# A hybrid transformer layer on one core: a small tile ahead of the feed-forward weights' buffers is made 96 bytes wider

## The chip, the core and the metric

The kernel runs on one core of one Trainium2 chip. A core has a matrix engine (TensorE; its matmuls are PE in the profile, its weight loads PEld), a vector engine (VectorE, DVE), a scalar engine (ScalarE, ACT), a third elementwise engine (GpSimd, POOL) and a queue that issues the transfers (SyncE, SP). They work on a local memory of 128 partitions; matmuls write to a separate accumulation memory (PSUM). The metric is the device time of one execution in microseconds, lower is better.

## The reference, cut to what matters

One layer of a diffusion backbone: 512 latent tokens and 256 context tokens of width 2048. Attention and a recurrence share one input and one output projection; then comes the feed-forward part, and a last norm:

```python
x = x + g1 * (jnp.concatenate([attn, rw], axis=-1) @ w_out)
x = x + g2 * swiglu(modulate(rmsnorm(x, norm2_g), sh2, sc2), ffn_w1, ffn_w3, ffn_w2)
...
def swiglu(h, w1, w3, w2):
    return (jax.nn.silu(h @ w1) * (h @ w3)) @ w2
```

Here h is 512 x 2048, w1 and w3 are 2048 x 5632, w2 is 5632 x 2048, all in 32-bit floats.

## The kernel before

Every large matrix product is made in three passes. Each factor is split into a high part, rounded to the matrix engine's reduced 32-bit format (F32R), and a low part, the rest; the helper `mm3` (lines 110, 113 and 114) issues three matmuls into one PSUM tile: high weights by high input, high weights by low input, low weights by high input. A matmul has a stationary operand of 128 x 128 (the weights, 512 bytes per partition, brought in by a weight load of its own) and a moving operand of 128 x 512 (the input, 2048 bytes per partition). Every matmul has its weight load, the second one of a triple too, though its weights are those of the first.

The weights of the feed-forward part come through `split2` (lines 1257 to 1266): a transfer fills one of four `raw` buffers (L1262), ACT casts it to `whi` (L1264, two buffers), and DVE subtracts, which gives `wlo` (L1265, two buffers). `raw`, `whi` and `wlo` are tiles of the pool `wf`. The input's parts `ahi` and `alo` are tiles of 16 x 512 per partition in the pool `xp`.

The feed-forward part goes in four rounds (`FCH`) over the hidden width. In a round, 11 blocks of w1 and w3 are made one after the other: per block 2 PSUM tiles `ps_u` with 16 steps of three matmuls each, so 96 matmuls a block and 1056 a round. ACT and DVE make the gated product of the two, split into `ghi` and `glo` (pool `gp`). Then come 16 tiles `ps_d` of the product with w2, of 11 steps of three matmuls, so 528 matmuls a round; DVE adds each to `x1`. In the first round DVE also works off rows of the modulation (`arow`, which use `raw` buffers). In the first block of the first round (L1283 on) the input `ahi`, `alo` is still being made. After the fourth round come a norm and 16 output transfers.

Two earlier stages use `mm3` with the same shapes: the input projection (`ps_z`; input `hhi` and the tiles `lo`, weights `whi` and `wlo` of the pool `wp`), and the last part of the output projection (`ps_o`; weights and input are slices of `ahi` and `alo`).

Within a pool, tiles lie one after the other in the order in which they are first made, each rounded up to a multiple of 32 bytes, and pools that are open together are stacked on each other. In the built program of the kernel before, the tiles that matter lie at these bytes of every partition:

| stage | stationary operand: start byte | modulo 128 | modulo 512 | moving operand: start byte | modulo 128 | modulo 512 |
|---|---|---|---|---|---|---|
| `ps_z` | `whi` 131008, 135104; `wlo` 139200, 143296 | 64 | 448 | `hhi` 49088; `lo` from 81856 on | 64 | 448 |
| `ps_o` | slices of `ahi` 49088 and `alo` 81856 | 64 | 448 | the same two tiles | 64 | 448 |
| `ps_u` | `whi` 153696, 159328; `wlo` 164960, 170592 | 96 | 96 | `ahi` 49088; `alo` 81856 | 64 | 448 |
| `ps_d` | `whi` and `wlo` as in `ps_u` | 96 | 96 | `ghi` 176224; `glo` 198752 | 96 | 96 |

One step of the contraction moves the stationary operand on by 512 bytes and the moving one by 2048, so both columns of remainders hold for every step. `gs2` lies at 126912 (64 bytes wide); after it in the same pool come three tiles of 16 bytes and two buffers `th` of 2048 bytes, and then `wf` begins with `raw` at 131168.

Of the kernel before, what the change touches and what calls it, by code (L numbers as in the profile page):

```python
# [10 lines left out]
F32 = mybir.dt.float32  # L11
# [9 lines left out]
P = 128  # L21
D = 2048
KT = D // P
# [40 lines left out]
def hybrid_layer_kernel(ctx: ExitStack, tc: tile.TileContext, xT, ctxT, pcol, ada_w, ada_t, w_in, lora_up, w_out, w13, w2,  # L64
# [14 lines left out]
    def pc(name, i=0, n=1):  # L79
        o = PC[name][0]  # L80
        return par[:, o + i:o + i + n]
# [652 lines left out]
    with ExitStack() as rc:  # L734
# [465 lines left out]
        wk = fc.enter_context(tc.tile_pool(name="wk", bufs=2, reuse_waits="tile"))  # L1200
# [52 lines left out]
    with fc:  # L1253
# [11 lines left out]
                eng.tensor_tensor(lo[:, :n], raw[:, :n], hi[:, :n].bitcast(F32), op=ALU.subtract)  # L1265
            return hi, lo

        gs2 = wk.tile([P, KT], F32, name="gs2", bufs=1)
        nc.vector.scalar_tensor_tensor(gs2, modT[:, 64:80, 0], 1.0, pc("n2g", 0, 16), op0=ALU.add, op1=ALU.mult)
        rs = ms.rstd(ps_f.tile([P, T], F32, tag="o", name="ps_rs"))  # L1270
        for k in range(KT):
# [177 lines left out]
```

## Time and profile before

| | |
|---|---|
| three runs | 3333.99 us median, 3332.64 to 3337.11 |
| the profiled execution | 3328.19 us |
| its span, first to last instruction | 3326.4 us |
| mean granted clock of TensorE over the span | 0.974 of full speed |
| busy share of PE, PEld, DVE, ACT, POOL | 95%, 74%, 52%, 35%, 17% |
| the feed-forward part | from 1830 us to 3304.5 us, then 21.9 us of norm and output |

The busy time of an engine is the time in which at least one of its instructions runs. Matmuls overlap in the engine: a duration runs from the issue of a matmul to its modelled end, so a matmul of 389 ns can be followed by the next one 227 ns after its start. What a run of matmuls costs is therefore read from the distance of their starts, or from a stretch without idle time divided by the number of its matmuls.

### The profile page before, as it was taken

Reading aid. Unit: us, or ns where it says so; the run is one execution under the profiler, and the core shown is the slowest. Engines: PE = TensorE matmul, PEld = TensorE weight load, DVE = VectorE, ACT = ScalarE, POOL = GpSimd, SP = SyncE. Lnnn points to the kernel's source line nnn. Section 1 sums busy time; section 2 is a strip of 40 time slices with the busy share of each in tenths; the row PEclk is TensorE's granted clock in tenths of the full one; section 3 lists DMA queues with packets and bytes.
Section 4 is the critical chain, followed back from the end, with each engine's and each line's share of the span. In section 5 each row is a group of like instructions: output and inputs, shape, how many; then the busy total and the mean of one; then the engine's idle time right before and its main releaser. Section 6 shows DMA issues by size and latency. Waiting matters only on the chain.

```text
span 3326.4 us, 49781 instructions
## 1 busy us (share of the span) xinstructions
PE 3161.6 (95%) x19840; PEld 2468.2 (74%) x19840; DVE 1743.5 (52%) x2906; ACT 1161.0 (35%) x2007; POOL 561.0 (17%) x597
## 2 busy tenths in 40 slices
PE   8989889989998999999997999999999999999997
PEld 4576557767775777777776788888888888888886
DVE  3377764576656777888885653323333232323233
ACT  4213333444344555555553422212221222112221
POOL 0000000253427344434433100000000000000011
PEclk9999999999999999999998999999999999999999
DMA  9675552354536345455465353322232223222232
GB/s 326 242 237 173 182 165 77 108 144 125 138 102 187 105 125 156 141 151 152 127 189 174 128 193 125 103 85 94 92 107 89 95 92 107 94 88 92 93 111 79
DMA packets 270920, 448.41 MB, mean 135 GB/s; under 512 B 109408, under 2 KB 156768, under 8 KB 270688
## 3 DMA queue, kind: packets, MB, share of 16 engines
q1 hardware_dynamic: 270688, 445.22, 42.9%
q8 instruction: 157, 2.57, 0.3%
q14 instruction: 75, 0.61, 0.1%
HBM read 383.52 MB, written 61.60 MB: 134 GB/s over the span
## 4 chain that ended last, share of the span: by engine, by line
PE 60%; DVE 4%; DMA 2%; POOL 1%; issue 1%; SPq 1%; ACT 0%; DVEq 0%; ACTq 0%; POOLq 0%
PE ps_u L114 10%; PE ps_u L113 10%; PE ps_u L110 10%; PE ps_d L113 5%; PE ps_d L110 5%; PE ps_d L114 5%; PE ps_x L852 2%; PE ps_m L982 2%; PE ps_y L863 2%; PE ps_op L110 2%; PE ps_i L901 2%; PE ps_op L114 1%; PE ps_op L113 1%; PE ps_i L907 1%; PE ps_w L971 1%; PE ps_c L1008 1%
## 5 line engine op out<-in xcount | busy, mean ns | idle before, releaser
L1264 ACT ACTIVATE whi<-raw 128x1024 fp32r<-128x1024 f32 (+1 forms) x240 | 275.0, 1146 | 1109.0 <-PE ps_u L113 603.8
L1265 DVE TENSOR_TENSOR wlo<-raw,whi 128x1024 fp32r<-128x1024 f32 (+1 forms) x238 | 317.9, 1336 | 501.2 <-ACT whi L1264 500.5
L114 PE MATMUL ps_u<-ahi,wlo 128*128 128x512 f32 x1408 | 563.0, 400 | 1.2 <-DVE wlo L1265 1.2
L113 PE MATMUL ps_u<-alo,whi 128*128 128x512 f32 x1408 | 556.1, 395 | 0.9 <-DVE alo L1280 0.9
L110 PE MATMUL ps_u<-ahi,whi 128*128 128x512 f32 x1408 | 552.6, 393 | 4.6 <-ACT whi L1264 2.9
L113 PEld LDWEIGHTS ps_u<-alo,whi 128*128 128x128 f32 x1408 | 265.0, 188 | 70.5 <-DVE alo L1280 1.6
L110 PEld LDWEIGHTS ps_u<-ahi,whi 128*128 128x128 f32 x1408 | 265.2, 188 | 69.1 <-ACT whi L1264 4.2
L114 PEld LDWEIGHTS ps_u<-ahi,wlo 128*128 128x128 f32 x1408 | 265.1, 188 | 62.9 <-DVE wlo L1265 2.0
L205 POOL TENSOR_TENSOR sq<-sq 128x512 f32<-128x512 f32 x22 | 40.8, 1855 | 1428.1 <-ACT sq L201 1427.8
L113 PE MATMUL ps_d<-glo,whi 128*128 128x512 f32 x704 | 273.3, 389 | 0.0
L110 PE MATMUL ps_d<-ghi,whi 128*128 128x512 f32 x704 | 273.3, 389 | 0.0
L114 PE MATMUL ps_d<-ghi,wlo 128*128 128x512 f32 x704 | 273.2, 389 | 0.0
L110 PE MATMUL ps_z<-hhi,whi 128*128 128x512 f32 x544 | 230.7, 424 | 7.6 <-DVE r__3128 L309 4.0
L114 PE MATMUL ps_z<-hhi,wlo 128*128 128x512 f32 x544 | 220.1, 405 | 16.8 <-DVE wlo L106 16.8
L113 PE MATMUL ps_z<-lo,whi 128*128 128x512 f32 x544 | 219.5, 403 | 0.0
L171 DVE SCALAR_TENSOR_TENSOR arow<-arow,siluB 128x1024 f32<-128x1024 f32 x128 | 156.4, 1223 | 116.2 <-DMA arow<-ada_t 115.6
L1315 DVE SCALAR_TENSOR_TENSOR x<-ps_d,modT,x 128x512 f32<-128x512 f32 x64 | 48.1, 751 | 299.8 <-PE ps_d L114 299.8
L893 POOL TENSOR_TENSOR bdB<-XY,mk 64x256 f16<-64x256 f32 x192 | 149.3, 777 | 171.7 <-DVE XY L854 156.0
L106 DVE TENSOR_TENSOR wlo<-raw,whi 128x1024 fp32r<-128x1024 f32 x80 | 106.3, 1329 | 92.3 <-ACT whi L105 92.1
L110 PEld LDWEIGHTS ps_d<-ghi,whi 128*128 128x128 f32 x704 | 132.1, 188 | 27.6
L114 PEld LDWEIGHTS ps_d<-ghi,wlo 128*128 128x128 f32 x704 | 132.1, 188 | 27.5
L113 PEld LDWEIGHTS ps_d<-glo,whi 128*128 128x128 f32 x704 | 132.1, 188 | 27.4
(624 smaller groups left out, 5770.4 us busy)
## 6 DMA issues: line engine op xcount, KB each, us to landing
raw<-w SPq DMA_DIRECT2D x176, 512.0 KB, 3.5
arow<-ada_t SPq DMA_DIRECT2D x128, 512.0 KB, 4.2
raw<-w SPq DMA_DIRECT2D x64, 704.0 KB, 4.1
raw<-w_in SPq DMA_DIRECT2D x72, 512.0 KB, 4.1
ada<-ada_w SPq DMA_DIRECT2D x64, 512.0 KB, 6.7
p1d<-pr SPq DMA_DIRECT2D x64, 256.0 KB, 2.8
XB<-bkd SPq DMA_DIRECT2D x96, 128.0 KB, 3.2
pr<-p1d SPq DMA_DIRECT2D x48, 256.0 KB, 3.2
```

Of the source, the lines that this page charges most:

```text
L106: nc.vector.tensor_tensor(lo, raw, hi.bitcast(F32), op=ALU.subtract)
L110: mm = nc.tensor.matmul(ps, lhsT=whi, rhs=hhi, start=first, stop=False)
L113: nc.tensor.matmul(ps, lhsT=whi, rhs=hlo, start=False, stop=False)
L114: nc.tensor.matmul(ps, lhsT=wlo, rhs=hhi, start=False, stop=last)
L171: nc.vector.scalar_tensor_tensor(a, a, 1.0, siluB[:, 1024 * h:1024 * h + 1024], op0=ALU.mult, op1=ALU.mult, accum_out=macc[:, j - 32, h:h ...
L852: nc.tensor.matmul(px[:, u, :], lhsT=AL[:, d, s_ + u, :], rhs=XB[:, d, s_ + u, :], start=True, stop=True)
L863: nc.tensor.matmul(py[m, u, :n], lhsT=XB[:, d, u, 64 * h:64 * h + P][:, m], rhs=GRz[h][:, d, u, :n], start=True, stop=True)
L893: nc.gpsimd.tensor_tensor(diag(B[l], h, d), ab[h][:, d], lm(l, h, d), op=ALU.mult)
L901: nc.tensor.matmul(ps[:, d, u, :], lhsT=lhs[:, d, u, :], rhs=rhs[:, d, u, :], start=True, stop=True)
L982: nc.tensor.matmul(pm[m, u, :n], lhsT=WT[e][h][:, d, u, m], rhs=YB[h][:, d, u, :n], start=True, stop=True)
L1264: nc.scalar.activation(hi[:, :n], raw[:, :n], AF.Copy)
L1265: eng.tensor_tensor(lo[:, :n], raw[:, :n], hi[:, :n].bitcast(F32), op=ALU.subtract)
```

## The change

The tile `gs2` (16 scales of the second norm per partition) is allocated with 24 further elements of 4 bytes, and only its first 16 elements are used, as before. No instruction is added, removed or given another shape or operand.

```diff
-        gs2 = wk.tile([P, KT], F32, name="gs2", bufs=1)
+
+        gs2 = wk.tile([P, KT + 24], F32, name="gs2", bufs=1)[:, :KT]
```

`gs2` is then 160 bytes wide in place of 64, a multiple of 32 in both cases. All that lies behind it moves up by 96 bytes: the three small tiles and `th` in `wk`, all of `wf` (`raw`, `whi`, `wlo`) and all of `gp` (`ghi`, `glo`). Their starts go from 96 to 64 modulo 128 (`whi`, `wlo`, `ghi` and `glo` from 96 to 192 modulo 512). `x1`, `ahi` and `alo` lie ahead of it and stay.

## Rows read from the trace of the kernel before

**Rows 1.** Page, parts 1 and 4: busy time, and the chain that ended last.

```profile
PE 3161.6 (95%) x19840; PEld 2468.2 (74%) x19840; DVE 1743.5 (52%) x2906; ACT 1161.0 (35%) x2007; POOL 561.0 (17%) x597
...
PE 60%; DVE 4%; DMA 2%; POOL 1%; issue 1%; SPq 1%; ACT 0%; DVEq 0%; ACTq 0%; POOLq 0%
PE ps_u L114 10%; PE ps_u L113 10%; PE ps_u L110 10%; PE ps_d L113 5%; PE ps_d L110 5%; PE ps_d L114 5%; PE ps_x L852 2%; PE ps_m L982 2%; PE ps_y L863 2%; PE ps_op L110 2%; PE ps_i L901 2%; PE ps_op L114 1%; PE ps_op L113 1%; PE ps_i L907 1%; PE ps_w L971 1%; PE ps_c L1008 1%
```

**Rows 2.** Busy time by stretch, first round: first block, other ten blocks.

```profile
core 0: us, PE busy (x) PEld busy (x) DVE busy (x) ACT busy (x) POOL busy (x), PEclk, DMA share, GB/s
1830.03:1863.08 33.05, 28.09 (x99) 20.56 (x100) 23.67 (x35) 21.57 (x28) 9.80 (x7) 0.87 0.09 32
1863.08:2086.38 223.30, 223.30 (x958) 179.65 (x957) 101.11 (x129) 52.60 (x60) 0.00 (x0) 1.00 0.51 166
```

**Rows 3.** Busy time by stretch: ps_d and ps_u in turn, end of the span.

```profile
2086.38:2206.10 119.72, 119.72 (x529) 99.10 (x528) 38.17 (x33) 22.34 (x18) 0.00 (x0) 1.00 0.27 91
2206.10:2452.52 246.42, 246.42 (x1058) 198.24 (x1057) 74.54 (x76) 57.65 (x66) 0.00 (x0) 1.00 0.30 97
...
2938.37:3184.78 246.41, 246.41 (x1057) 198.23 (x1056) 74.52 (x76) 57.64 (x66) 0.00 (x0) 1.00 0.30 97
3184.78:3304.50 119.72, 119.72 (x529) 99.10 (x528) 36.94 (x32) 29.12 (x31) 29.28 (x14) 1.00 0.21 70
3304.50:3326.40 21.90, 3.94 (x25) 3.47 (x23) 14.45 (x32) 0.63 (x1) 0.00 (x0) 0.62 0.52 192
```

**Rows 4.** Groups by line and shape, 1863 to 3304 us: matmuls and weight loads.

```profile
line engine op names shapes xcount | busy us, mean ns | idle before us <-releasers
L114 PE MATMUL ps_u<-ahi,wlo 128*128 128x512 f32 x1376 | 549.1, 399 | 0.5 <-DVE wlo L1265 0.5
L113 PE MATMUL ps_u<-alo,whi 128*128 128x512 f32 x1375 | 541.8, 394 | 0.0
L110 PE MATMUL ps_u<-ahi,whi 128*128 128x512 f32 x1375 | 539.0, 392 | 0.0
L110 PE MATMUL ps_d<-ghi,whi 128*128 128x512 f32 x704 | 273.3, 389 | 0.0
L113 PE MATMUL ps_d<-glo,whi 128*128 128x512 f32 x703 | 272.9, 389 | 0.0
L114 PE MATMUL ps_d<-ghi,wlo 128*128 128x512 f32 x703 | 272.8, 389 | 0.0
```

**Rows 5.** Timeline of PE in the input projection: start us, us, line, operands.

```profile
874.52 0.39 PE L110 MATMUL ps_z<-hhi,whi 128*128 128x512 f32 x1
874.75 0.39 PE L113 MATMUL ps_z<-lo,whi 128*128 128x512 f32 x1
...
877.92 0.39 PE L110 MATMUL ps_z<-hhi,whi 128*128 128x512 f32 x1
```

**Rows 6.** The tile ps_o: duration ns min/median/max, first and last start.

```profile
L113 PE MATMUL ps_o<-alo,ahi x27: 389/389/628, 1800.7 to 1819.8; 128*128 128x512 f32 x27
L114 PE MATMUL ps_o<-ahi,alo x27: 387/389/628, 1801.2 to 1820.0; 128*128 128x512 f32 x27
```

**Rows 7.** Groups by line and shape: casts and subtractions of both weight paths.

```profile
L106 DVE TENSOR_TENSOR wlo<-raw,whi 128x1024 fp32r<-128x1024 f32 x80 | 106.3, 1329 | 92.3 <-ACT whi L105 92.1
...
L1265 DVE TENSOR_TENSOR wlo<-raw,whi 128x1024 fp32r<-128x1024 f32 x174 | 213.8, 1229 | 457.5 <-ACT whi L1264 456.8
L1264 ACT ACTIVATE whi<-raw 128x1024 fp32r<-128x1024 f32 x176 | 186.5, 1060 | 743.1 <-PE ps_u L113 570.7 <-issue 134.0 <-PE ps_d L113 37.5
```

**Rows 8.** Waits, 1863 to 3304 us: total us, times, longest.

```profile
ACT whi L1264 <- PE ps_u L113: 594.3, 139, 4.5
...
DVE arow L171 <- DMA arow<-ada_t: 46.4, 26, 3.7
```

**Rows 9.** The tile raw, 1826 to 3304 us: its transfers, issue to landing.

```profile
DMA to landing us min/median/max: 3.3/3.6/6.2
```

## The prediction

> **What bounds the kernel now.** I read the page first. PE is busy for 95% of the span, and the chain that ended last runs through PE for 60%; of that the feed-forward matmuls alone make some 45% (three lines of `ps_u` at 10% each, three of `ps_d` at 5%) [rows 1]. The change touches only what lies behind `gs2`, so I then cut the feed-forward part into its stretches, with the busy time of each engine. What is to be seen there: but for the first block, PE's busy time equals the length of every stretch to 0.01 us, at a granted clock of 1.00 (the upper level, 2.4 GHz), while DVE and ACT are busy for a half and less [rows 2, 3]. From 1863 to 3304.5 us the time is therefore the number of matmuls times the distance between their starts, and nothing else.
>
> That distance is not the same in the two halves of a round. A `ps_u` stretch has 1056 matmuls (11 blocks of 96, from the code; the counts in the rows also take in a matmul or two at the edges) and takes 246.42 us: 233.35 ns a matmul. A `ps_d` stretch has 528 and takes 119.72 us: 226.74 ns [rows 3]; the three full stretches of the one kind and the four of the other agree to 0.01 us. Shapes, types, clock and weight loads are alike. The groups by line say the same in durations: 392, 394 and 399 ns for the three matmuls of a `ps_u` step, 389 ns for each of the three of `ps_d` [rows 4]. The excess over 389 adds up to 18 ns a step, and the distances give 3 x 6.61 = 19.8 ns; I take the distances.
>
> So 6.61 ns a matmul are lost in `ps_u`, and the question is to what. The table of addresses offers one answer: in `ps_u` the weights start at 96 modulo 128 bytes and the input at 64, in `ps_d` both start at 96. Two earlier stages are the control, because they share with `ps_u` the place of the input (bytes 49088 and 81856 on) and the same helper, but have weights at 64. In the input projection 15 matmuls in a row start from 874.52 to 877.92 us [rows 5]: 3.40 us / 15 = 226.7 ns, as in `ps_d`. In the last part of the output projection the low parts' matmuls have a median of 389 ns [rows 6]. `ps_z` also has 16 steps a tile, as `ps_u` has, so the number of steps is not what sets the two apart. Three stages with one offset cost 226.7 ns or 389 ns, whether that offset is 64 or 96; the one stage with two offsets costs more. I read this as reads of one operand that get in the way of the other's when they are not in step, since the next weights are loaded while the input streams; the trace shows the cost, not that reason.
>
> **The change part by part.**
>
> *`ps_u`, all but the first block.* The weights move from 96 to 64 modulo 128, where `ahi` and `alo` are. Matmuls concerned: 957 in the first round (1056 less the 99 that start by 1863.08 us [rows 2]) and 3 x 1056 = 3168 in the others, 4125 in all. They take 223.30 + 246.42 + 246.42 + 246.41 = 962.55 us now [rows 2, 3]. At the distance of `ps_d` and `ps_z` they would take 4125 x 226.74 ns = 935.30 us. Gain: 27.25 us. Nothing waits in these stretches, so PE gets all of it, and everything behind moves up with it. Bounds: no gain, if the offset is not the reason; and no more than this, since the trace has no `mm3` stage whose 512-column matmuls come at less than 226.7 ns in a run.
>
> *`ps_u`, the first block.* PE is busy for 28.09 of 33.05 us at a mean granted clock of 0.87 [rows 2] and waits for the input and the weights in between. 99 x 6.61 ns = 0.65 us is the most that can come back; I take 0, since that block ends with its last weights.
>
> *`ps_d`.* `whi`, `wlo`, `ghi` and `glo` all move by 96 bytes, so they go on sharing one offset, now 64 instead of 96. `ps_z` has 64 for both and the same distance. I take 0; the bounds are 0 as far as 64 and 96 are concerned.
>
> *Casts, subtractions and transfers at the new addresses.* These are hidden behind the matmuls. The nearest row for buffers at 64 is the path of the input projection, where the subtraction takes 1329 ns against 1229 here [rows 7]; there is other work on DVE there, and I take no difference. If the 100 ns were due to the address: the cover is the time for which ACT waits for a buffer to come free, 594.3 us in 139 waits, 4.3 us each [rows 8]. A half block (24 matmuls) gets shorter, from 24 x 233.35 = 5.60 us to 5.44 us, and the cast, the subtraction and one row of the modulation on DVE (1.06 + 1.23 + 1.23 us) still fit in it. Without that cover, all 176 subtractions of 1024 elements would cost 17.6 us. The transfers take 3.6 us from issue to landing, at most 6.2 [rows 9], with four `raw` buffers ahead; DVE's 26 waits for `arow` (46.4 us) [rows 8] are off the path, PE having no idle time there. Nothing more is asked of the transfers but 3% more rate. No instruction is added.
>
> *Waits on older tiles.* A tile waits until those that held its bytes before are released. By the addresses, each moved tile overlaps the same earlier tiles in its old and its new place, so no wait comes or goes.
>
> Sum: 3328.19 - 27.25 = 3300.94 us for an execution like the profiled one. That one is 5.8 us (0.17%) below the median of the three runs, for reasons that lie outside this part; so against the median, 3333.99 - 27.25 = **3306.7 us**, 0.8% faster.
>
> **The rivals.**
>
> *No change: the address has no part in it.* The Trainium skill speaks for this one, on the page "SBUF — State Buffer", section "Who interferes with whom": TensorE has two read ports of its own, one for the moving operand and one for weight loads, and never waits on anyone. By that rule the sum would be 0 and the time 3334.0 us. The rows speak against it, for 233.35 and 226.74 ns stand in one and the same part of the kernel, at one clock, over thousands of matmuls [rows 3, 4]; something tells them apart, and in `ps_z` the number of steps, the place of the input and the shapes are those of `ps_u`. Against my reading: `ps_u` differs from the others also in that its PSUM tiles alternate in pairs, and in where its weights lie at large. 3334.0 us.
>
> *Part of it.* The third matmul of a step has an excess of 10 ns in its duration, the first 3 and the second 5 [rows 4]. If one kind of pairing is cured and another is not, 3 to 15 of the 18 ns remain: a gain of a sixth to five sixths, 4.5 to 22.7 us; in the middle 3320 us.
>
> *Slower: the offsets must agree modulo 512, not 128.* All three good stages agree modulo 512 too (448 and 448, or 96 and 96), a weight tile being 512 bytes wide. After the change the weights are at 192 and the input at 448: 256 apart, farther from agreement than now (160). The trace has no stage with that distance. If it makes all three matmuls of a step as dear as the dearest is now, 10 ns over `ps_d` instead of a mean excess of 6 ((3 + 5 + 10) / 3) [rows 4], each of the 4125 costs 4 ns more: +16.5 us, 3350.5 us. It decides as soon as the distance between starts in `ps_u` is above 233.35 ns. For it speaks only that the rows can't tell 128 from 512; against it, that a rule modulo 64, 128 or 256 would fit the rows as well and give the full gain, and that even modulo 512 a distance of 256 may be harmless or only cost a part.
>
> **How the numbers follow.** The full gain 0.78; part of it 0.07; no change 0.08; slower 0.07. Differences under 0.2% (6.7 us) are about what a measurement of this kernel can't tell from no change. Faster then takes the full gain and nearly all of the partial one, 0.84; same takes no change and the smallest partial ones, 0.09; slower 0.07. The range has to hold the full gain with the spread of the runs (1.4 us below the median, 3.1 above it) and the upper bound of the first block: 3306.7 - 1.4 - 0.65, with some 2 us for another set of runs, gives 3302; above, 3309.8 for the highest run, and on to 3318 for partial gains from 16 us up. That leaves out the other partial cases, no change and slower, 2 in 10.
>
> **What would show it.** In the profile after: `ps_u` stretches of 239.4 us in rounds two to four (1056 x 226.74) and near 217 us for the ten blocks of the first; all three `ps_u` groups at 389 ns; `ps_d` stretches still at 119.7 us; the first block still about 33 us; PE without idle time in between, and ACT's waits for `ps_u` shorter by about 0.16 us each. Wrong it would be if `ps_u` keeps 392, 394 and 399 ns (the address is not the reason), if the three change unequally (it is, but not by this remainder alone), if `ps_d` gets dearer, or if the matmuls get faster and idle time appears before `whi` or `wlo`.

## The result, and the profile after

The changed kernel takes 3306.79 us (median of four runs, 3305.69 to 3311.38) against 3334.01 us before; the ratio is 0.9921, with a 95% interval of 0.9905 to 0.9936. So it is faster by 0.8%, and the time is that of the forecast, 3306.7 us. That the two agree to 0.1 us is luck, since runs of either kernel spread over more than 4 us; what bears the forecast out is the stretches below.

The execution of the changed kernel that was profiled is the slowest of its four (3311.38 us, span 3309.6 us): its feed-forward part begins at 1840.76 us in place of 1830.03. The instructions ahead of that point are the same in both kernels and their tiles have not moved. In the profiles shown below the same point lies between 1830 and 1850 us, also for kernels that differ only behind it. I therefore compare stretches of the feed-forward part, which repeat to some 0.02 us, and not spans.

Busy time by stretch in the profile after, cut as in [rows 2, 3] (first block; the other ten blocks of the first round; then `ps_d` and `ps_u` in turn; the end):

```profile
core 0: us, PE busy (x) PEld busy (x) DVE busy (x) ACT busy (x) POOL busy (x), PEclk, DMA share, GB/s
1840.76:1873.83 33.07, 28.25 (x100) 21.04 (x101) 23.70 (x35) 21.55 (x28) 9.78 (x7) 0.85 0.10 32
1873.83:2090.76 216.93, 216.93 (x958) 179.54 (x957) 100.96 (x129) 52.60 (x60) 0.00 (x0) 1.00 0.51 170
2090.76:2210.44 119.68, 119.68 (x529) 99.10 (x528) 38.14 (x33) 22.34 (x18) 0.00 (x0) 1.00 0.27 92
2210.44:2449.80 239.36, 239.36 (x1057) 198.20 (x1056) 74.51 (x76) 57.53 (x66) 0.00 (x0) 1.00 0.30 100
...
2928.52:3167.88 239.36, 239.36 (x1058) 198.20 (x1056) 74.51 (x76) 57.52 (x66) 0.00 (x0) 1.00 0.30 100
3167.88:3287.56 119.68, 119.68 (x529) 99.10 (x528) 36.92 (x32) 29.08 (x31) 29.21 (x14) 1.00 0.21 70
3287.56:3309.60 22.04, 4.07 (x25) 3.60 (x23) 14.44 (x32) 0.63 (x1) 0.00 (x0) 0.57 0.51 190
```

Here is the whole gain. Each full `ps_u` stretch went from 246.42 to 239.36 us, 226.67 ns a matmul instead of 233.35, and the ten blocks of the first round from 223.30 to 216.93 us. PE still has no idle time in these stretches. The rest stands where it was: `ps_d` 119.68 us (119.72 before), the first block 33.07 us (33.05), the end 22.04 us (21.90). The feed-forward part and the end together went from 1496.4 to 1468.8 us, which is 27.5 us.

The groups by line of the profile after, 1874 to 3288 us, answer to [rows 4]:

```profile
L113 PE MATMUL ps_u<-alo,whi 128*128 128x512 f32 x1375 | 534.9, 389 | 0.0
L114 PE MATMUL ps_u<-ahi,wlo 128*128 128x512 f32 x1375 | 534.9, 389 | 0.0
L110 PE MATMUL ps_u<-ahi,whi 128*128 128x512 f32 x1375 | 534.9, 389 | 0.0
L113 PE MATMUL ps_d<-glo,whi 128*128 128x512 f32 x704 | 273.2, 389 | 0.0
```

The three matmuls of a `ps_u` step, 392, 394 and 399 ns before, have become alike and as short as those of `ps_d`. What hides behind them did not move. The first row is from the waits of the profile after over the same stretch, the second from its groups by line and shape; they answer to [rows 7, 8]:

```profile
ACT whi L1264 <- PE ps_u L113: 571.2, 139, 4.4
```

```profile
L1265 DVE TENSOR_TENSOR wlo<-raw,whi 128x1024 fp32r<-128x1024 f32 x174 | 213.7, 1229 | 437.9 <-ACT whi L1264 437.2
```

ACT waits 0.17 us less for each buffer (571.2 us in 139 waits, 594.3 before), which is what a half block got shorter by. The subtraction takes 1229 ns at the new address too.

### The profile page after: what moved, and what is told of

Read it like the earlier page. It is cut to its first block, busy times and chain, and to the rows that moved or that the text cites. A ratio compares the mean times of both kernels' runs of the same rounds, so it can differ in the third digit from the quotient of the medians.

```text
span 3309.6 us, 49781 instructions
## 1 busy us (share of the span) xinstructions
PE 3140.8 (95%) x19840; PEld 2470.5 (75%) x19840; DVE 1742.7 (53%) x2906; ACT 1160.5 (35%) x2007; POOL 561.2 (17%) x597
## 4 chain that ended last, share of the span: by engine, by line
PE 59%; DVE 4%; DMA 2%; POOL 2%; issue 1%; ACT 1%; SPq 0%; DVEq 0%; ACTq 0%; POOLq 0%
PE ps_u L114 10%; PE ps_u L113 10%; PE ps_u L110 10%; PE ps_d L110 5%; PE ps_d L113 5%; PE ps_d L114 5%; PE ps_m L982 2%; PE ps_x L852 2%; PE ps_y L863 2%; PE ps_op L110 2%; PE ps_i L901 2%; PE ps_op L114 1%; PE ps_op L113 1%; PE ps_w L971 1%; PE ps_i L907 1%; PE ps_c L1008 1%
## 5 line engine op out<-in xcount | busy, mean ns | idle before, releaser
L114 PE MATMUL ps_u<-ahi,wlo 128*128 128x512 f32 x1408 | 549.4, 390 | 1.2 <-DVE wlo L1265 1.2
```

Of the source, the lines that this page charges most:

```text
L114: nc.tensor.matmul(ps, lhsT=wlo, rhs=hhi, start=False, stop=last)
```

## The experiments

The profile after shows that the move took the excess away. It doesn't show which remainder counts, whether the same would happen in another stage, or which pairs of operands must agree. All kernels below move buffers by widening tiles, as the change does. "Distance" is the start of the weights less the start of the input, and a stage is called free when its matmuls start 226.7 ns apart, as those of `ps_d` did before. Apart from the first and the last two, these kernels ran once, so their stretches are compared and not their whole times. In each fence the first row is a full `ps_u` stretch (1056 matmuls), the second a full `ps_d` stretch (528), from the view by stretch: us, PE's busy time with the number of its instructions, granted clock, share of the DMA engines, GB/s.

**The first product's distance put into the second** (the kernel before, with this edit):

```diff
-        ghi = gp.tile([P, FPC, T], F32R, name="ghi")
-        glo = gp.tile([P, FPC, T], F32R, name="glo")
+        ghi = gp.tile([P, FPC * T + 32], F32R, name="ghi")[:, 24:24 + FPC * T].rearrange("p (k t) -> p k t", t=T)
+        glo = gp.tile([P, FPC * T + 32], F32R, name="glo")[:, 24:24 + FPC * T].rearrange("p (k t) -> p k t", t=T)
```

> The kernel before, with the inputs of the second product (ghi, glo) moved up by 96 bytes, so that its weights start 32 bytes past its input modulo 128, as those of the first product do. First theory, the offset between weights and input sets the distance of the matmuls' starts in any stage: a full ps_d stretch goes from 119.72 to 528 x 233.35 ns = 123.2 us, its three kinds to 392, 394 and 399 ns, the kernel from 3334.0 to 3348 us (four stretches of 3.5 us). Second theory, the dearer matmuls belong to the stage ps_u itself (its PSUM tiles, or where its buffers lie at large): ps_d stays at 119.7 us and 389 ns, the kernel at 3334 us.

```profile
2225.17:2471.58 246.41, 246.41 (x1057) 1.00 0.30 97
2471.58:2594.78 123.20, 123.20 (x529) 1.00 0.26 89
```

`ps_d` went to 123.20 us, the predicted 123.2, and the kernel to 1.0034 of the time before (interval 1.0020 to 1.0048); the four stretches of 3.5 us are 14 us or 1.0042, which lies in it. The second theory falls: a stage that the change never touched gets as dear as `ps_u` was, by a move of its inputs alone. It is the relation of the two addresses, not the stage. One thing was not expected: the three kinds of matmul of `ps_d` became 396, 395 and 397 ns, not 392, 394 and 399. Widening `ghi` by 128 bytes also put `glo` 128 further on modulo 256; I took no notice of that, since I thought in remainders of 128. In this kernel and the next three, the distance that is stated for `ps_d` holds modulo 128 only.

**64 and 96**: `gs2` wider by 32 bytes, `ghi` and `glo` shifted by 32 as in the first edit.

> gs2 wider by 32 bytes: in ps_u the weights start 64 bytes past the input modulo 128; ghi and glo moved up by a further 32: in ps_d the weights start 96 past the input (that is 32 ahead of it). If only equality modulo 128 is free: a full ps_u stretch near 246.4 us as before, a ps_d stretch near 123.2 us. If modulo 64 is what counts: ps_u 239.4 us, as after the change, and ps_d 123.2 us. If the stage itself is the reason: 246.4 and 119.7 us.

```profile
2213.39:2455.11 241.72, 241.72 (x1058) 1.00 0.31 99
2455.11:2578.29 123.18, 123.18 (x529) 1.00 0.27 89
```

**96 and 64**: the same with 64 and 64.

> gs2 wider by 64 bytes and ghi and glo moved up by a further 64: the same two distances exchanged, 96 in ps_u and 64 in ps_d. If only equality modulo 128 is free: ps_u near 246.4 us, ps_d near 123.2 us. If modulo 64 is what counts: ps_u 246.4, ps_d 119.7 us. Were a distance of 96 to cost otherwise than one of 32, ps_u here and ps_d of the kernel with 64 and 96 must show the same size for each matmul.

```profile
2228.04:2474.44 246.40, 246.40 (x1058) 1.00 0.31 97
2474.44:2596.09 121.65, 121.65 (x529) 1.00 0.27 90
```

Modulo 64 is refuted by both: at a distance of 64 neither stage is free. It is cheaper there than elsewhere, 241.72 / 1056 = 228.9 ns and 121.65 / 528 = 230.4 ns, against 233.3 at 96 in both stages. So "any distance costs the same" is wrong as well. It is not 64 as such that is cheap: modulo 512 the distance in `ps_u` is 192 here, and one of 64 costs 233.3 ns in a kernel further down.

**128 and 112**: `gs2` wider by 224 bytes, `ghi` and `glo` shifted by 16.

> gs2 wider by 224 bytes: in ps_u weights and input agree modulo 128 but are 128 apart modulo 256; ghi and glo moved up by a further 16: in ps_d the weights start 112 past the input (16 ahead of it). If modulo 128 is what counts: ps_u 239.4 us, as after the change; if modulo 256: ps_u dearer than that, up to 246.4 us or more. For ps_d: if any distance costs the same, 123.2 us; if the cost grows with the distance, between 119.7 and 123.2 us; if units of 32 bytes decide, 119.7 us or 123.2 us and nothing between.

```profile
2219.29:2464.69 245.40, 245.40 (x1058) 1.00 0.30 97
2464.69:2586.71 122.02, 122.02 (x530) 1.00 0.27 90
```

This is the run that changes the reading. Weights and input of `ps_u` agree modulo 128, as in the changed kernel, and the stretch still takes 245.40 us (232.4 ns a matmul). Agreement modulo 128 is not enough. `ps_d` came to 122.02 us, between the free value and the dear one; since `ghi` lies 16 bytes past the weights and `glo` 144, the run can't say which of the three forecasts for it holds.

**Agreement modulo 512, and 128 once more.** From here on the inputs' and weights' tiles are widened by 512 bytes when they are shifted, so that the distance holds for all of a stage's operands.

```diff
-        gs2 = wk.tile([P, KT], F32, name="gs2", bufs=1)
+        gs2 = wk.tile([P, KT + 88], F32, name="gs2", bufs=1)[:, :KT]
...
+        ghi = gp.tile([P, FPC * T + 128], F32R, name="ghi")[:, 32:32 + FPC * T].rearrange("p (k t) -> p k t", t=T)
+        glo = gp.tile([P, FPC * T + 128], F32R, name="glo")[:, 32:32 + FPC * T].rearrange("p (k t) -> p k t", t=T)
```

> gs2 wider by 352 bytes: in ps_u weights and input agree modulo 512 (the change has them 256 apart); ghi and glo moved up by 128: in ps_d they agree modulo 128 and are 128 apart modulo 256. If agreement modulo 256 is what counts: ps_u 239.4 us, ps_d dearer than 119.7 us, near 528 x 232.4 ns = 122.7 us. If modulo 128: 239.4 and 119.7 us. If modulo 512 were better still than 256: ps_u under 239.3 us.

```profile
2208.30:2447.67 239.37, 239.37 (x1057) 1.00 0.31 100
2447.67:2570.86 123.19, 123.19 (x529) 1.00 0.27 90
```

Agreement modulo 512 gives what 256 gives (239.37 and 239.36 us). A distance of 128, now the same for `ghi` and `glo` and in the other stage, costs the full 123.19 us. Modulo 128 is refuted twice.

**32 and 64; 96 and 16**: `gs2` wider by 384 and 448 bytes, `ghi` and `glo` shifted by 448 and 496.

> gs2 wider by 384 bytes and ghi, glo moved up by 448: in ps_u the weights start 32 bytes past the input modulo 512, in ps_d 64 past. If agreement modulo 256 alone is free, both are dearer than 226.7 ns a matmul: ps_u between 241 and 247 us, ps_d between 120.8 and 123.5 us. If the sign of the distance matters (weights ahead or behind), one of these small distances past the input could be as good as 0 or better: ps_u at or under 239.4, ps_d at or under 119.7 us.

```profile
2215.15:2461.54 246.39, 246.39 (x1058) 1.00 0.30 97
2461.54:2584.74 123.20, 123.20 (x529) 1.00 0.27 89
```

> gs2 wider by 448 bytes and ghi, glo moved up by 496: in ps_u the weights start 96 bytes past the input modulo 512, in ps_d 16 past. If agreement modulo 256 alone is free: ps_u between 241 and 247 us, ps_d between 120.8 and 123.5 us. If units of 32 bytes decide, 16 is free or as dear as 32 and nothing between. If the cost shrinks with the distance, ps_d lies between 119.7 and what 64 costs.

```profile
2218.60:2466.00 247.40, 247.40 (x1057) 1.00 0.30 97
2466.00:2590.93 124.93, 124.93 (x529) 1.00 0.26 87
```

No small distance past the input is as good as none, and the cost does not shrink with the distance: 16 bytes are the dearest case of all, 124.93 / 528 = 236.6 ns, so units of 32 bytes don't decide either. Both stretches of this last kernel are above the ranges that were expected (247 and 123.5 us). Together, for the distances that hold for all operands, in ns a matmul (stretch over number of matmuls):

| distance modulo 512 | 0 | 16 | 32 | 64 | 96 | 128 or 384 | 160 | 192 | 224 | 256 |
|---|---|---|---|---|---|---|---|---|---|---|
| `ps_u` | 226.7 | | 233.3 | | 234.3 | 232.4 | 233.3 | 228.9 | 233.3 | 226.7 |
| `ps_d` | 226.7 | 236.6 | | 233.3 | | 233.3 | | | | |

(160 is the kernel before, 256 the change; `ps_u` and `ps_d` at 384 are the two runs with 128.) Only 0 and 256 are free among those tried.

**The low weights alone off by 32** (the changed kernel, with `wlo` starting 32 bytes into a tile widened by 512, and `ghi`, `glo` shifted by 32):

```diff
-            lo = wf.tile([P, WT], F32R, tag="wlo", name="wlo")
+            lo = wf.tile([P, WT + 128], F32R, tag="wlo", name="wlo")[:, 8:8 + WT]
```

> The changed kernel with the low parts of the weights alone moved up by 32 bytes, and ghi, glo too. In ps_u the high weights agree with both inputs and the low ones are 32 past them; in ps_d the low weights agree and the high ones are 32 ahead. Theory of the neighbours: what costs is the weight load that runs while an input streams, so with the low weights off, the second matmul of a step (during which they are loaded) gets dearer; with the high weights off, the first and the third. Theory of the pair: a matmul pays for its own weights; then the third alone in ps_u, the first and second in ps_d. Either way a full ps_u stretch lies between 239.4 and 246.4 us (about 241.7 if a third of the excess stays), ps_d between 119.7 and 123.2 us (about 122.0). If one loss sets the phase for the matmuls behind it, all three kinds change, and neither pattern is seen.

```profile
2223.68:2470.05 246.37, 246.37 (x1057) 1.00 0.31 97
2470.05:2593.24 123.19, 123.19 (x530) 1.00 0.27 89
```

The durations by tile of this kernel (ns min/median/max), `ps_u`:

```profile
L110 PE MATMUL ps_u<-ahi,whi x1408: 387/395/796, 1845.6 to 3208.5; 128*128 128x512 f32 x176
L113 PE MATMUL ps_u<-alo,whi x1408: 392/400/793, 1847.7 to 3208.7; 128*128 128x512 f32 x176
L114 PE MATMUL ps_u<-ahi,wlo x1408: 388/389/629, 1848.3 to 3208.9; 128*128 128x512 f32 x176
```

Both sums are missed: with one of the two weight tiles off, the whole excess is there (246.37 us), not a part of it. Of the pattern, the second matmul is the dearest (400 ns) and the third, the only one whose own weights are off, is free (389 ns); the first is dearer too (395 ns), which neither theory said. The pattern can't decide between them, though, since it is not set by the distances alone. In the kernel of the first experiment nothing of `ps_u` had moved, and its stretch took 246.41 us (246.42 before). Yet there the dearest matmul is the second, where in the kernel before it was the third [rows 4]:

```profile
L110 PE MATMUL ps_u<-ahi,whi x1408: 392/394/792, 1847.0 to 3210.1; 128*128 128x512 f32 x176
L113 PE MATMUL ps_u<-alo,whi x1408: 392/399/796, 1849.1 to 3210.3; 128*128 128x512 f32 x176
L114 PE MATMUL ps_u<-ahi,wlo x1408: 389/392/628, 1849.7 to 3210.6; 128*128 128x512 f32 x176
```

**Two pairs in turn.** `mm3` is replaced in both products by three matmuls a step that take two pairs in turn, and `alo`, `wlo` and `glo` are shifted by 32 bytes against `ahi`, `whi` and `ghi`, which agree modulo 512:

```diff
+        def in_turn(ps, pairs, first, last):
+            for i in range(3):
+                w, x = pairs[turn[0] % 2]
+                turn[0] += 1
+                nc.tensor.matmul(ps, lhsT=w, rhs=x, start=first and i == 0, stop=last and i == 2)
...
-                    mm3(ps, whi[:, k * P:(k + 1) * P], wlo[:, k * P:(k + 1) * P], ghi[:, k, :], glo[:, k, :],
-                        k == 0, k == FPC - 1)
+                    in_turn(ps, ((whi[:, k * P:(k + 1) * P], ghi[:, k, :]),
+                                 (wlo[:, k * P:(k + 1) * P], glo[:, k, :])), k == 0, k == FPC - 1)
```

and in `ps_u` with the pairs `whi`, `alo` and `wlo`, `ahi`.

> Both feed-forward products with the matmuls of two pairs in turn (three a step as before, so the products are not the reference's: high by low and low by high in ps_u, high by high and low by low in ps_d). One pair's operands lie 32 bytes from the other's. In ps_d each matmul's own weights and input agree, and the weights loaded during it, those of the next, do not agree with its input. In ps_u it is the other way round: own weights and input 32 apart, the next weights in agreement with the input that streams. Theory of the neighbours (the load that runs while an input streams is what it must agree with): ps_u 239.4 us, ps_d near 123.2 us. Theory of the pair (a matmul's own weights and input): ps_u near 246.4 us, ps_d 119.7 us.

```profile
2217.75:2460.64 242.89, 242.89 (x1057) 1.00 0.31 98
2460.64:2583.78 123.14, 123.14 (x529) 1.00 0.27 89
```

The control has the same turn with no shift:

> The same two pairs in turn with every operand at one offset modulo 512. Both theories: ps_u 239.4 us, ps_d 119.7 us; anything else is due to the order of the pairs itself.

```profile
2217.63:2456.99 239.36, 239.36 (x1058) 1.00 0.31 100
2456.99:2576.67 119.68, 119.68 (x530) 1.00 0.28 92
```

The control is free in both stages, so the turn itself costs nothing. With the shift, `ps_d`, where each matmul's own operands agree and only the next weights do not, pays the full price (233.2 ns). The theory of the pair falls. `ps_u`, where the next weights agree and only the own do not, pays half (230.0 ns), where the theory of the neighbours had forecast no excess (239.4 us). So that theory is not the whole either. What holds is this: a matmul's input has to agree with the weights that are loaded while it streams. When they are loaded is to be seen in this kernel's timelines of PE and PEld, here in `ps_d`:

```profile
2500.02 0.39 PE L1294 MATMUL ps_d<-glo,wlo 128*128 128x512 f32 x1
2500.25 0.39 PE L1294 MATMUL ps_d<-ghi,whi 128*128 128x512 f32 x1
```

```profile
2500.02 0.19 PEld L1294 LDWEIGHTS ps_d<-ghi,whi 128*128 128x128 f32 x1
2500.25 0.19 PEld L1294 LDWEIGHTS ps_d<-glo,wlo 128*128 128x128 f32 x1
```

The load for a matmul starts with the matmul before it. What the half in `ps_u` is paid for stays open. With two pairs in turn, a matmul's own weights have the same offset as those of the next but one, whose load starts with the next matmul, when the record of this one (0.39 us) has not ended. The run can't tell a relation to its own weights from one to these.

**Once more, beside a wider pad.** The first has `gs2` wider by 352 bytes and nothing else, the second is the changed kernel.

> gs2 wider by 352 bytes in place of 96: all weights and inputs of the feed-forward part agree modulo 512. If agreement modulo 256 is all that counts: ps_u 239.4 us, ps_d 119.7 us, ratio to the kernel before 0.992, as for the change. If the last step from 256 to 512 brings something: under 0.991.

> The changed kernel as it is, beside the one with 352 bytes: 0.992 of the kernel before, both within 0.1% of each other if 256 or 512 makes no difference.

The ratios to the kernel before are 0.993 (interval 0.9912 to 0.9948) and 0.992 (0.9898 to 0.9942), and full stretches take 239.36 and 119.68 us in both. The medians, 3311.8 and 3309.2 us, are 0.08% apart, as expected; the runs of either kernel spread over more than that. A version that beats the change was not found: none of the distances tried is better than 0.

## Why the prediction was right

- **What bounds it.** That PE is the only limit of these stretches held: the matmuls got cheaper, and the time fell by their sum. No idle time came up before `whi` or `wlo`.
- **The size.** 6.61 ns for each of 4125 matmuls, 27.25 us, was read off from the distance between the two halves of a round. Measured: (223.30 - 216.93) + (739.26 - 3 x 239.36) = 6.37 + 21.18 = 27.55 us. (The three full stretches before are 246.42, 246.43 and 246.41 us; the prediction took 246.42 for the second.) The small remainder is that `ps_u` came to 226.67 ns and not 226.74: the full `ps_d` stretch of before, from which that price was taken, was itself 0.04 us longer than after. Those 0.04 us lie at its start. Right behind the dear matmuls of `ps_u`, some of its own were still dear, up to 397 ns until 2088.5 us, as the row for one line shows; from there on all three kinds stand at 389 ns, as they do from the start after the change.

```profile
L113 PE MATMUL ps_d<-glo,whi x3: 393/397/397, 2086.6 to 2088.0; 128*128 128x512 f32 x3
```

- **The edits costed at nothing.** First block 33.07 against 33.05 us, the subtraction 1229 ns at both addresses, no change in what is transferred: all as forecast. `ps_d`, moved with all its operands, stayed.
- **No change: the address has no part in it.** Refuted, most plainly by the first experiment, which makes `ps_d` dear by moving its inputs. The Trainium skill, page "SBUF — State Buffer", section "Who interferes with whom", has TensorE's two reads independent and never waiting. The time that follows from it, no change, is not what was measured: the same matmul takes 226.7 to 236.6 ns at different distances. That it is these two reads that wait for each other no run shows.
- **Part of it.** Did not happen: all three kinds came to 389 ns. Its price, and that of the rival below, was taken from the excess of each kind (3, 5 and 10 ns), as if each kind belonged to one pairing. The first experiment shows that it does not: there the excess moved from kind to kind with the addresses of `ps_u` unchanged.
- **Slower: modulo 512.** Refuted by the result, since 256 apart is free.
- **What was too wide in the reading.** The prediction took the column "modulo 128" of the addresses as the reason and said that modulo 64, 128 or 256 would fit as well. The experiments leave only 256: a distance of 128 costs 232.4 and 233.3 ns. The prediction was right on this point by luck: the 96 bytes of the change were enough because they happen to make the distance 256; a pad of 224 bytes, which also makes the starts agree modulo 128, would have given almost nothing (245.40 us a stretch against 246.42).
- **What stays open.** Reads in each other's way, as a mechanism, was only argued. The runs show a relation between the input that streams and the weights loaded meanwhile, and half of its cost where these agree and a matmul's own weights do not. They don't show what that half is paid for, why 16 bytes cost more than 64, why one weight tile off costs as much as two, why 128 costs 232.4 ns in one stage and 233.3 in the other, or whether 256 is the period at distances that were not tried.

## What to carry to other kernels

Where a long stretch of matmuls has no idle time, divide its length by their number and compare it with another stretch of the same shapes: a few ns that differ at the same clock are worth looking for in the addresses. For the 32-bit reduced format with a weight load for each matmul, let weights and streaming input start at one offset modulo 256 bytes, and make sure of it for every tile that is loaded while another streams; here one low-order tile off by 32 bytes cost as much as all of them. A remark such as "modulo 128" is tested by a second pad that fits it as well, before the rule is used elsewhere.

## What the runs showed of the hardware that was not expected

- Distance 0 or 256 bytes (modulo 512) between weights and input: 226.67 ns from start to start of 128 x 512 matmuls at a granted clock of 1.00 (2.4 GHz). Others: 228.9 ns (192), 232.4 to 234.3 ns (32 to 160, 224), 236.6 ns (16).
- Where the loss falls need not follow the program. In the kernel with a distance of 128 the dear matmuls go through all three lines of a step in turn, as its timeline of PE shows (start us, us, line, operands):

```profile
2300.62 0.39 PE L114 MATMUL ps_u<-ahi,wlo 128*128 128x512 f32 x1
2300.85 0.40 PE L110 MATMUL ps_u<-ahi,whi 128*128 128x512 f32 x1
2301.09 0.40 PE L113 MATMUL ps_u<-alo,whi 128*128 128x512 f32 x1
2301.33 0.40 PE L114 MATMUL ps_u<-ahi,wlo 128*128 128x512 f32 x1
2301.56 0.39 PE L110 MATMUL ps_u<-ahi,whi 128*128 128x512 f32 x1
...
2302.48 0.40 PE L113 MATMUL ps_u<-alo,whi 128*128 128x512 f32 x1
2302.71 0.40 PE L114 MATMUL ps_u<-ahi,wlo 128*128 128x512 f32 x1
2302.95 0.40 PE L110 MATMUL ps_u<-ahi,whi 128*128 128x512 f32 x1
```

  Three dear ones begin at the first matmul of a step, and three more, 1.63 us later, at the second. The operands of a line have the same distance each time, so what a matmul pays depends also on how the ones before it went. A mean by line therefore does not say which pairing is to blame; the distance of starts over a long stretch gives at least the whole loss.
- Matmuls whose weights and input agree can be dear for a while too. The run of `ps_z` from which the prediction took its 15 matmuls begins with six more. Of those the first, the second and the fourth still last 0.40 us (timeline of the kernel before):

```profile
873.14 0.40 PE L110 MATMUL ps_z<-hhi,whi 128*128 128x512 f32 x1
873.37 0.40 PE L113 MATMUL ps_z<-lo,whi 128*128 128x512 f32 x1
873.61 0.39 PE L114 MATMUL ps_z<-hhi,wlo 128*128 128x512 f32 x1
873.84 0.40 PE L110 MATMUL ps_z<-hhi,whi 128*128 128x512 f32 x1
```

  In front of them stands a run of other matmuls, of 256 columns. So 226.7 ns is the price of a run that has settled. The start of `ps_d` before the change is another such case.
